# One of the last stores of a short-sequence attention kernel, sent out in three pieces of 49, 49 and 30 rows

## Chip, cores, metric

One core of one Trainium2 chip. The metric is device time in microseconds (us) of the whole program; each number is the median of several executions, or a single one where the text says so.

## The reference

```python
q, k, v: (32, 12, 128, 64) float32
scale = 1.0 / np.sqrt(q.shape[-1])
scores = scale * np.matmul(q, k.transpose(0, 1, 3, 2))
attn = np.exp(scores - scores_max)
attn = attn / (np.sum(attn, axis=-1, keepdims=True) + 1e-8)
return np.matmul(attn, v).astype(np.float32)
```

384 heads of 128 x 64. The kernel works in 24 chunks of 16 heads.

## The kernel before

A chunk's result is one tile in SBUF, the on-chip memory: 128 partitions (rows) with 4 KB each. Its store moves these 128 rows of 4 KB (512 KB) to HBM, the main memory. Stores are held back while loads run, and go out in groups of three at the end:

```python
def store(c, eng):
    o_sb, _ = osbs.pop(c)
    eng.dma_start(out=orr[:, c, :], in_=o_sb.rearrange("p t d -> p (t d)"))

e = NCH - 1                                   # 23
held = {c: [c - LAG] if c >= LAG else [] for c in range(e - 4)}
# ... (cut: held[e - 4] to held[e - 2])
held[e - 1] = [e - 5, e - 4, e - 3]           # stores 18, 19, 20
held[e] = [e - 2, e - 1, e]                   # stores 21, 22, 23
# ... (cut: the chunk loop)
    for s in held[c]:
        store(s, nc.scalar if s < e - 2 else nc.sync)
```

Stores up to 20 are issued from ScalarE, the last three from SyncE. Each store uses one of eight completion semaphores, in rotation, and waits until the store that had it before has landed. All loads but two at the start are issued from GpSimd and cast to bf16 on the way.

The softmax here doesn't subtract the row's maximum and nothing guards it: scores larger than these inputs give would overflow.

## Time and profile before

| | before |
|---|---|
| median | 130.61 us (130.34 to 130.7, 3 runs) |
| span of the profiled execution | 128.6 us |
| last exp on ScalarE | 114.95 to 116.84 us |
| stores 18, 19, 20 issued | 115.03, 115.47, 116.18 us |
| stores 21, 22, 23 issued | 114.62, 118.82, 121.92 us |
| last landing of store 23 | 127.35 us |

The prediction below shows the lines of this profile. The core has 16 DMA engines; a store of 128 rows gives 8 rows to each, and the store has landed when the slowest of the 16 is done. The engines reach SBUF through *ports*, each of which serves a group of partitions; the prediction names the page that tells of them.

Two things are read from the trace below the level of the page. *Landings* are the single semaphore increments, one for each DMA engine that a store used. *Row records* are the single 4 KB packets with start and duration; 159 ns is the usual one, and a *long record* here is one well above that. A new record of an engine starts 3 or 4 ns before its last one ends, so that records can be linked into one chain for each engine. That linking is a reconstruction: the ends of the chains are firm, while two chains may have been swapped further back. The tables of chains below therefore also ask that the rows between the increments of one queue fit the stores: 8 of a whole store, and 7, 7 and 2 of the three pieces.

### The profile page before, as it was taken

To read this page: it belongs to the slowest core of one execution; us is meant where nothing else is said; L and a number is where in the kernel's file an instruction comes from. 1 tells how busy PE (TensorE), PEld (TensorE's weight loads), DVE (VectorE), ACT (ScalarE), POOL (GpSimd) and SP (SyncE) were. 2 spreads that over 40 slices of the span, in tenths; PEclk is the share of its full clock that TensorE was granted. 3 is DMA by queue.
4 is the path that set the end of the run, shared out by engine and by line. 5 is a ranking of instruction groups with operands and counts; after the bars stand their busy time and mean duration, and the time that the engine had idled before them with its cause. 6 is when DMAs were issued, how large, how long until landed. Compare 5 with 4: busy or idle time off the path is not lost.

```text
span 128.6 us, 4637 instructions
## 1 busy us (share of the span) xinstructions
PE 69.7 (54%) x2080; PEld 42.7 (33%) x2080; DVE 85.7 (67%) x150; ACT 71.8 (56%) x74; POOL 79.5 (62%) x88
## 2 busy tenths in 40 slices
PE   0036966577546757775636296190976663684000
PEld 0025644444223433443314144050544331552000
DVE  0380398584879678979958669464799997777500
ACT  3216588669658737875774486371757775523000
POOL 6951314235699986998738487808999952355300
PEclk9999999999999977999999959968689998555555
DMA  3999999999999999999999999999999999999982
GB/s 118 312 194 186 210 204 204 209 213 202 216 202 209 207 215 206 207 212 209 283 290 269 221 284 207 286 287 209 287 210 285 287 285 325 389 418 414 419 364 83
DMA packets 16723, 32.27 MB, mean 251 GB/s; under 512 B 1344, under 2 KB 7488, under 8 KB 16704
## 3 DMA queue, kind: packets, MB, share of 16 engines
q0 software_dynamic: 12960, 18.35, 80.1%
q10 hardware_dynamic: 3168, 11.54, 23.0%
q1 hardware_dynamic: 576, 2.10, 4.2%
q8 instruction: 16, 0.26, 0.7%
q14 instruction: 3, 0.02, 0.0%
HBM read 37.75 MB, written 12.58 MB: 391 GB/s over the span
## 4 chain that ended last, share of the span: by engine, by line
DMA 58%; DVE 12%; POOL 11%; PE 6%; issue 4%; ACT 1%; POOLq 0%; DVEq 0%; ACTq 0%
DMA k_bf<-in_k_dram 33%; DMA q_bf<-in_q_dram 11%; DMA v_bf<-in_v_dram 11%; DVE o_sb L178 6%; POOL o_sb L183 4%; POOL v_bf L65 4%; PE s_ps L120 3%; DMA out_dram<-o_sb 3%; DVE kt L109 3%; DVE qt L107 2%; POOL q_bf L58 2%; PE o_ps L159 2%; ACT attn L124 1%; DVE o_sb L186 1%; PE v_ps L139 1%
## 5 line engine op out<-in xcount | busy, mean ns | idle before, releaser
L124 ACT ACTIVATE attn<-s_ps 128x2048 bf16<-128x2048 f32 x24 | 45.1, 1877 | 38.2 <-PE s_ps L120 33.2
L183 POOL TENSOR_TENSOR o_sb<-o_sb,recip 128x1024 f32<-128x1024 f32 x23 | 43.9, 1915 | 8.7 <-DVE o_sb L178 8.5
L178 DVE STREAM_TRANSPOSE o_sb<-o_ps 128x512 f32<-128x512 f32 x48 | 33.1, 711 | 14.3 <-PE o_ps L159 13.2
L139 PE MATMUL v_ps<-v_bf,perm 128*32 128x512 bf16 (+1 forms) x448 | 33.5, 405 | 3.4 <-DMA v_bf<-in_v_dram 3.4
L120 PE MATMUL s_ps<-qt,kt 32*128 32x128 bf16 x768 | 17.2, 232 | 33.1 <-DVE kt L109 33.1
L143 ACT CAST v<-v_ps 128x512 bf16<-128x512 f32 x48 | 26.4, 589 | 2.6 <-PE v_ps L139 2.4
L120 PEld LDWEIGHTS <-kt 32*128 32x128 bf16 x768 | 12.6, 100 | 43.1 <-DVE kt L109 42.5
L159 PE MATMUL o_ps<-attn,v 128*32 128x128 bf16 x768 | 22.4, 245 | 2.7 <-issue 2.7
L58 POOL DMA_DIRECT2D k_bf<-in_k_dram x23 | 12.3, 536 | 15.5 <-DMA v_bf<-in_v_dram 10.8
L171 DVE STREAM_TRANSPOSE dt<-d_ps 128x512 f32<-128x512 f32 x24 | 16.3, 678 | 6.4 <-PE d_ps L149 6.4
L109 DVE STREAM_TRANSPOSE kt<-k_bf 128x512 f32<-128x512 f32 x24 | 16.3, 680 | 5.5 <-DMA k_bf<-in_k_dram 5.4
L159 PEld LDWEIGHTS <-v 128*32 128x32 bf16 x768 | 15.7, 108 | 11.4 <-issue 6.5
L58 POOL DMA_DIRECT2D q_bf<-in_q_dram x23 | 13.5, 585 | 6.4 <-DMA v_bf<-in_v_dram 3.7
L107 DVE STREAM_TRANSPOSE qt<-q_bf 128x512 f32<-128x512 f32 x24 | 16.2, 673 | 1.6 <-DMA q_bf<-in_q_dram 1.5
L149 PE MATMUL d_ps<-attn,ones 128*32 128x512 bf16 x96 | 11.4, 453 | 9.5 <-ACT attn L124 9.5
L65 POOL DMA_DIRECT2D v_bf<-in_v_dram x12 | 9.1, 760 | 9.3 <-DMA k_bf<-in_k_dram 3.4
L139 PEld LDWEIGHTS <-perm 128*32 128x32 bf16 x448 | 12.1, 110 | 5.0 <-issue 2.6
L149 PEld LDWEIGHTS <-ones 128*32 128x32 bf16 x96 | 4.7, 104 | 15.8 <-issue 12.9
L173 DVE RECIPROCAL recip<-dt 128x16 f32<-128x16 f32 x24 | 6.1, 254 | 1.9
L83 DVE CAST q_bf<-raw 128x1024 bf16<-128x1024 f32 x1 | 0.8, 815 | 5.3 <-DMA raw<-in_q_dram 5.3
L83 ACT CAST k_bf<-raw 128x1024 bf16<-128x1024 f32 x1 | 1.0, 1046 | 3.0 <-DMA raw<-in_k_dram 3.0
L83 ACT ACT_TABLE_LOAD x1 | 1.3, 1283 | 1.2 <-PEq L244 1.2
(11 smaller groups left out, 3.8 us busy)
## 6 DMA issues: line engine op xcount, KB each, us to landing
out_dram<-o_sb ACTq DMA_DIRECT2D x21, 512.0 KB, 7.4
v_bf<-in_v_dram POOLq DMA_DIRECT2D x12, 512.0 KB, 13.8
q_bf<-in_q_dram POOLq DMA_DIRECT2D x23, 256.0 KB, 13.4
k_bf<-in_k_dram POOLq DMA_DIRECT2D x23, 256.0 KB, 13.2
out_dram<-o_sb SPq DMA_DIRECT2D x3, 512.0 KB, 6.4
raw<-in_k_dram ACTq DMA_DIRECT2D x1, 512.0 KB, 4.7
raw<-in_q_dram SPq DMA_DIRECT2D x1, 512.0 KB, 4.6
```

Of the source, the lines that this page charges most:

```text
L58: nc.gpsimd.dma_start(out=x, in_=src[:, c, :].rearrange("p (t d) -> p t d", t=TQ))
L107: nc.vector.transpose(xt.rearrange("p h (x g) -> p x h g", g=GQ), x)
L109: nc.vector.transpose(xt.rearrange("p h (x g) -> p x h g", g=GQ), x.rearrange("p (y t) e -> p t y e", y=2))
L120: nc.tensor.matmul(s_ps[:, b, h, :], lhsT=kt[pr, h, :, j], rhs=qt[pr, h, :, j], start=(j == 0), stop=(j == 1), tile_position=(b * 32, 0))
L124: nc.scalar.activation(out=attn, in_=s_ps, func=mybir.ActivationFunctionType.Exp, bias=0.0, scale=scale)
L139: nc.tensor.matmul(v_ps[u * 32:(u + 1) * 32, i], lhsT=perm[:, a + i, tl, :], rhs=v_bf[:, ns, 2 * u + tl, :], start=(tl == 0), stop=(tl == ...
L143: nc.scalar.copy(v2s[m][:, a:a + heads, ns], v_ps)
L149: nc.tensor.matmul(d_ps[b * 32:(b + 1) * 32], lhsT=ones, rhs=attns[c][:, b], start=True, stop=True, tile_position=(0, b * 32))
L159: nc.tensor.matmul(o_ps[b * 32:(b + 1) * 32, h], lhsT=v2s[c // 4][:, 4 * (b % 2) + h, 2 * (c % 4) + b // 2, j * 32:(j + 1) * 32], rhs=attn ...
L171: nc.vector.transpose(dt, turned(d_ps))
L178: nc.vector.transpose(o_sb[:, :, j * 32:(j + 1) * 32], turned(o_ps))
L183: nc.gpsimd.tensor_mul(o_sb, o_sb, recip.to_broadcast([128, TQ, D]))
```

## The change

The intent, as its sizes tell it: to take rows of one late store off the higher DMA engines and give them to the lower ones, so that all end together. It can be done only through the number of rows of a piece, because that number decides how many engines carry it.

```diff
+    UNEVEN = NCH - 4
@@
         def store(c, eng):
             o_sb, _ = osbs.pop(c)
-            eng.dma_start(out=orr[:, c, :], in_=o_sb.rearrange("p t d -> p (t d)"))
+            rows = (0, 49, 98, 128) if c == UNEVEN else (0, 128)
+            for lo, hi in zip(rows, rows[1:]):
+                eng.dma_start(out=orr[lo:hi, c, :],
+                              in_=o_sb[lo:hi].rearrange("p t d -> p (t d)"))
```

## The prediction

> **What bounds the kernel now.** I read the page's 40 slices first, then the engine busy times of the tail, then the waits of the SyncE queue, then the single landings of the last stores. In the slices the computing engines stop two to four slices before the end, while the DMA row stays full almost to the last slice (one slice is 128.6 / 40 = 3.2 us):
>
> ```profile
> DVE  0380398584879678979958669464799997777500
> ACT  3216588669658737875774486371757775523000
> POOL 6951314235699986998738487808999952355300
> PEclk9999999999999977999999959968689998555555
> DMA  3999999999999999999999999999999999999982
> ```
>
> The end is not compute: DVE and POOL end in slice 38 of 40. The tail cut into stretches (columns: stretch, its length, busy time of PE, PEld, DVE, ACT, POOL, granted clock, mean busy share of the 16 DMA engines, GB/s):
>
> ```profile
> 118.00:120.00 2.00, 0.35 (x15) 0.08 (x4) 1.86 (x5) 0.00 (x0) 1.47 (x2) 0.50 1.02 412
> 120.00:122.00 2.00, 0.00 (x0) 0.00 (x0) 0.92 (x1) 0.00 (x0) 0.37 (x1) 0.50 1.02 416
> 122.00:124.00 2.00, 0.00 (x0) 0.00 (x0) 0.00 (x0) 0.00 (x0) 0.00 (x0) 0.50 1.03 422
> 124.00:125.00 1.00, 0.00 (x0) 0.00 (x0) 0.00 (x0) 0.00 (x0) 0.00 (x0) 0.50 0.81 332
> 125.00:126.00 1.00, 0.00 (x0) 0.00 (x0) 0.00 (x0) 0.00 (x0) 0.00 (x0) 0.50 0.50 205
> 126.00:127.00 1.00, 0.00 (x0) 0.00 (x0) 0.00 (x0) 0.00 (x0) 0.00 (x0) 0.50 0.35 143
> 127.00:128.60 1.60, 0.00 (x0) 0.00 (x0) 0.00 (x0) 0.00 (x0) 0.00 (x0) 0.50 0.00 0
> ```
>
> No engine computes after 121 us; all 16 DMA engines are full until 124, then half of them (0.50), then a third, then none. So the last 3 us are an uneven finish, and the program ends only when the last store has landed:
>
> ```profile
> SPq L191 <- POOL o_sb L183: 17.4, 2, 13.6
> SPq L255 <- DMA out_dram<-o_sb: 4.9, 2, 4.0
> ```
>
> The second line is the closing wait of SyncE (a closing exchange of semaphores between the engines follows it, from the last landing at 127.35 to the end of the span at 128.6). The single semaphore increments of the last stores, one for each DMA engine, are in the trace; sorted, they fall into seven early, one in the middle and eight late (us from the span's start; stores numbered by chunk):
>
> | store | seven early | one | eight late |
> |---|---|---|---|
> | 19, ScalarE queue | 120.67 to 121.76 | 121.81 | 123.47 to 124.59 |
> | 20, ScalarE queue (the one changed) | 121.91 to 123.18 | 123.51 | 125.51 to 126.43 |
> | 23, SyncE queue (last) | 124.41 to 125.50 | 125.53 | 126.74 to 127.35 |
>
> The increments do not carry the engine's number. Seven early ones and a change that uses seven engines belong together: I take the early seven for engines 0 to 6. That is an inference, not a reading. A 4 KB row costs an engine 156 ns: increments of consecutive stores on one early engine lie 1,248 ns apart for 8 rows. The record of one row is 159 ns with sixteen engines running and the same 159 ns with eight, so the engines do not slow each other through a common limit.
>
> **What the Trainium skill says.**
> - "DMA: Bandwidth & Descriptors", section "Why a DMA increments its semaphore by 16 and not by 1": a store issued from ScalarE or SyncE uses the largest number up to 16 that divides its slowest dimension, on the lowest-numbered engines. So 49 rows go on engines 0 to 6 with 7 rows each, and 30 rows on 0 to 14 with 2 each. The trace agrees as far as it can: each 128-row store there shows 16 increments.
> - The same page, "Latency and other measured facts": engines 7 and 15 are usually the slower ones, by its best guess because of the descriptor rings of loads issued from GpSimd. The trace has the lag, but on eight engines, not two; it is there already when the last such loads land (104.7 to 109.3 us for one of them).
> - "SBUF — State Buffer", section "Door 1: The DMA port swizzle": rows 0 to 63 sit on eight ports and 64 to 127 on the other eight, a port gives about 27.2 GB/s, and it was measured that 64 partitions get hardly more than 32. One engine takes 4,096 / 156 ns = 26.3 GB/s here, so one engine nearly fills one port. The trace of before has no two engines on one port on purpose, so it can't show what sharing costs.
>
> **The change part by part.** It removes one 128-row store of 8 rows on each of 16 engines, and adds three.
> 1. *Rows by engine.* Engines 0 to 6: 7 + 7 + 2 = 16 rows, 8 more. Engines 7 to 14: 2 rows, 6 fewer. Engine 15: none, 8 fewer. Sum 7 x 16 + 8 x 2 = 128, as before.
> 2. *Ends.* Early engines: 8 x 0.156 = 1.25 us later, so 125.66 to 126.75. Late engines: 6 x 0.156 = 0.94 us earlier, 125.80 to 126.41 (engine 15 0.31 us more). The middle one, if it is engine 7, ends at 124.6. The last landing moves from 127.35 to 126.75: **0.60 us saved**. The rest of the closing, 1.25 us, stays.
> 3. *Two more issues.* One costs ScalarE's queue 0.34 us (median of its store issues). In the built kernel the first piece takes the semaphore of store 20, the second that of store 15, the third that of store 16, and each waits until that store has landed: at 117.32 and 118.74. ScalarE computes nothing after 116.84, so the issues cost no compute. The early engines still have stores 19 and the first piece to carry until after 121 us, so the pieces are in the ring some 2 us before they are due. **0 us.**
> 4. *The three last stores.* Their semaphores are the same ones in both builds; the last one waits for store 21 to land (121.85), which is ahead of store 20 on the late engines. **0 us.** On TensorE, VectorE and GpSimd the instructions are in the same order.
>
> Sum: 130.61 - 0.60 = 130.0 us if a row costs the same on any engine. I take a third of that off for shared ports (below): **130.2 us**.
>
> **Rivals.**
> - *Ports, not engines.* Rows 64 to 127 sit on the eight ports that the late engines read through. After the change an early engine reads up to 34 of those 64 rows from the second piece, and more from the third, at a time (121 to 124) when the late engines read there without a pause. If the port is the limit, the rows of each port are as many as before and the late half gains nothing; an early engine that shares takes up to twice 156 ns for some 5 to 7 rows, at most 1.1 us: end at 127.3 to 127.8, time 130.6 to 131.0. For it: the skill's measurement and 26.3 against 27.2 GB/s. Against it: nothing in this trace. I give it 35%.
> - *The early seven are not engines 0 to 6.* If late engines are among them, they get 8 rows more: 127.35 + 1.25 = 128.6, time 131.9. For it: no increment names its engine, and the grouping is one execution's. Against it: the sizes of the change fit the seven. 10%.
> - *A late issue.* The pieces wait for stores 15 and 16; were these some 3 us later, engines 0 to 6 would run dry. Then the change gives back part of its 0.6 us: 130.3. 5%.
> - The chunk pipeline before 116 us, where loads set the pace, is not touched; a gain of more than 1.3 us could only come from there.
>
> **Range and chances.** The engine sum gives 130.0 (about half), the port rival 130.6 to 131.0, the wrong seven 131.9. The runs of before differ by 0.36 us. So 129.6 to 131.1 holds about 8 in 10. Two per cent is 2.6 us, twice the largest effect counted on either side: faster 0.02, same 0.95, slower 0.03.
>
> **What would show it.** Right: the DMA share of 124 to 126 rises from 0.5 to 0.8 or more, and falls to nothing by 126.8 instead of 127; the last store's landings close up, engine 7 apart, to a spread of about 1.1 us from 2.9; rows still take 159 ns. Ports: row records of 200 to 320 ns between 121 and 126, and the last landing at 127.3 or later. Wrong seven: a longer tail at a share of 0.5 or less. Late issue: a gap on seven engines, with full share lost before 124. The prediction fails if the load phase shifts between builds, so that stores begin their tail at another time than 116 us.

## The result and the profile after

| | before | after |
|---|---|---|
| median | 130.64 us (130.34 to 130.7, 4 runs) | 131.62 us (131.42 to 131.94, 4 runs) |
| ratio | 1 | 1.0082 (95%: 1.0055 to 1.0108) |
| last landing of store 23 | 127.35 us | 128.43 us |
| store 23 issued | 121.92 us | 121.90 us |
| row time beyond 159 ns a row, all engines, from 117 us | 0.6 us | 8.1 us |

A ratio is the mean time of one kernel's fast runs over that of the other's of the same rounds, so not quite the ratio of the medians. The kernel became about 0.8% slower, where 0.3% faster was forecast; 131.62 us is above the range of 129.6 to 131.1 us.

The tail of the changed kernel in the same stretches (stretch, length, busy time of PE, PEld, DVE, ACT, POOL, granted clock, mean busy share of the DMA engines, GB/s):

```profile
118.00:120.00 2.00, 1.16 (x36) 0.82 (x28) 1.54 (x4) 0.00 (x0) 1.60 (x1) 0.50 1.03 410
120.00:122.00 2.00, 0.00 (x0) 0.00 (x0) 1.69 (x2) 0.00 (x0) 1.04 (x1) 0.50 0.99 381
122.00:124.00 2.00, 0.00 (x0) 0.00 (x0) 0.00 (x0) 0.00 (x0) 0.00 (x0) 0.50 0.99 354
124.00:125.00 1.00, 0.00 (x0) 0.00 (x0) 0.00 (x0) 0.00 (x0) 0.00 (x0) 0.50 1.05 389
125.00:126.00 1.00, 0.00 (x0) 0.00 (x0) 0.00 (x0) 0.00 (x0) 0.00 (x0) 0.50 0.77 315
126.00:127.00 1.00, 0.00 (x0) 0.00 (x0) 0.00 (x0) 0.00 (x0) 0.00 (x0) 0.50 0.26 107
127.00:128.00 1.00, 0.00 (x0) 0.00 (x0) 0.00 (x0) 0.00 (x0) 0.00 (x0) 0.50 0.16 66
128.00:129.70 1.70, 0.00 (x0) 0.00 (x0) 0.00 (x0) 0.00 (x0) 0.00 (x0) 0.50 0.00 0
```

Part of the forecast is there: the share in 125 to 126 us rose from 0.50 to 0.77, and in 126 to 127 it fell from 0.35 to 0.26. Two things were not foreseen. From 127 to 128 us a share of 0.16 stays, two to three engines of sixteen. And between 120 and 124 us the engines are as busy as before (0.99) but move 381 and 354 GB/s, where before moved 416 and 422: busy time that moves less, which is what long row records look like in this view. The closing wait of SyncE for the last stores (us in total, times, longest) grew with it, from 4.9 us:

```profile
SPq L194 <- POOL o_sb L184: 17.7, 2, 14.0
SPq L259 <- DMA out_dram<-o_sb: 6.0, 2, 3.1
```

So two suspects stood at the start: **some of engines 0 to 6 are late ones** (called "wrong seven" in the expectations), and **shared SBUF ports**, which make rows long. Two more were kept as rivals: the two added issues with their semaphores, and the HBM side (an engine writes other output rows than before). The load phase did move a little between the two profiles: the last exp started at 115.76 us, 0.8 us later than before. The halves below show what that is worth: their last exp started at 115.74 us, and they end as before.

### The profile page after: what moved, and what is told of

The parts are those of the page before. It is cut to its first block, busy times and chain, and to the rows that moved or that the text cites. A ratio compares the mean times of both kernels' runs of the same rounds, so it can differ in the third digit from the quotient of the medians.

```text
span 129.7 us, 4639 instructions
## 1 busy us (share of the span) xinstructions
PE 70.6 (54%) x2080; PEld 42.9 (33%) x2080; DVE 85.3 (66%) x150; ACT 71.7 (55%) x74; POOL 79.6 (61%) x88
## 4 chain that ended last, share of the span: by engine, by line
DMA 58%; DVE 12%; POOL 11%; PE 7%; issue 3%; ACT 1%; ACTq 0%; POOLq 0%; DVEq 0%
DMA k_bf<-in_k_dram 34%; DMA q_bf<-in_q_dram 11%; DMA v_bf<-in_v_dram 11%; DVE o_sb L179 6%; POOL o_sb L184 4%; POOL v_bf L66 4%; PE s_ps L121 4%; DVE kt L110 3%; DMA out_dram<-o_sb 3%; DVE qt L108 2%; POOL q_bf L59 2%; PE o_ps L160 2%; ACT attn L125 1%; DVE o_sb L187 1%; PE v_ps L140 1%
## 5 line engine op out<-in xcount | busy, mean ns | idle before, releaser
L121 PE MATMUL s_ps<-qt,kt 32*128 32x128 bf16 x768 | 17.7, 237 | 33.0 <-DVE kt L110 33.0
L144 ACT CAST v<-v_ps 128x512 bf16<-128x512 f32 x48 | 26.3, 590 | 2.9 <-PE v_ps L140 2.9
L66 POOL DMA_DIRECT2D v_bf<-in_v_dram x12 | 9.3, 775 | 10.6 <-DMA k_bf<-in_k_dram 4.6
```

Source lines behind the costliest of these rows:

```text
L121: nc.tensor.matmul(s_ps[:, b, h, :], lhsT=kt[pr, h, :, j], rhs=qt[pr, h, :, j], start=(j == 0), stop=(j == 1), tile_position=(b * 32, 0))
L144: nc.scalar.copy(v2s[m][:, a:a + heads, ns], v_ps)
```

## The experiments

All kernels but one (nine more stores at the end) differ from the changed kernel, or from the one before, only in how store 20 (in one group stores 18 to 20) is cut, and three of them in the partitions that it reads. Those with a wrong result are named.

### Which part of the loss is issue, which is ports

**Columns.** Three pieces again, but each with all 128 rows, so that engines and ports are as before:

```diff
-            rows = (0, 49, 98, 128) if c == UNEVEN else (0, 128)
+            cols = (0, 6, 12, 16) if c == UNEVEN else (0, 16)
+            # out=orr[:, c, lo * D:hi * D], in_=o_sb[:, lo:hi]
```

> Store 20 in three pieces by columns (6, 6 and 4 of the 16 groups of 64): all 128 rows in each piece, so each engine keeps its own port and its own share, and only the number of issues and semaphores is that of the change. Shared ports, HBM side or counts as the cause: 130.5 to 130.9 us. Issue and semaphores: 131.4 to 131.9 us.

Measured: 130.76 us, 1.000 (0.9978 to 1.0022). Two more issues and their semaphores cost nothing that can be measured. That rival is out.

**Halves.** Every engine has its 8 rows, but two engines read through one port:

```diff
-            rows = (0, 49, 98, 128) if c == UNEVEN else (0, 128)
+            rows = (0, 64, 128) if c == UNEVEN else (0, 128)
```

> Store 20 as rows 0 to 63 and 64 to 127: each half over all 16 engines with 4 rows each, so every engine has 8 rows as before, but two engines read through one port. Shared ports: records of about 300 ns in both halves, time 130.9 to 131.8 us. Counts of rows by engine as the cause: 130.6 us, records of 159 ns. Issue and semaphores as the cause: about half the loss, 131.1 us, without long records.

Measured: 130.74 us, 1.0011 (0.998 to 1.0042). Long records are there (4.9 us beyond 159 ns in all, up to 639 ns), but the last landing is 127.46 us, as before. Its tail ends before 127.0 us, as before:

```profile
125.00:126.00 1.00, 0.00 (x0) 0.00 (x0) 0.00 (x0) 0.00 (x0) 0.00 (x0) 0.50 0.64 258
126.00:127.00 1.00, 0.00 (x0) 0.00 (x0) 0.00 (x0) 0.00 (x0) 0.00 (x0) 0.50 0.39 160
127.00:128.60 1.60, 0.00 (x0) 0.00 (x0) 0.00 (x0) 0.00 (x0) 0.00 (x0) 0.50 0.00 0
```

Shared ports alone, with equal rows, did not move the end. The expectation from ports missed.

**Even and odd ports.** The three pieces of the change, to the same output rows, but all read from partition 0 on, or all from partition 64 on (wrong results):

```diff
             for lo, hi in zip(rows, rows[1:]):
+                f = 0 if c == UNEVEN else lo        # second kernel: f = 64
                 eng.dma_start(out=orr[lo:hi, c, :],
-                              in_=o_sb[lo:hi].rearrange("p t d -> p (t d)"))
+                              in_=o_sb[f:f + hi - lo].rearrange("p t d -> p (t d)"))
```

> The same three pieces of store 20 on the same engines and to the same rows of the output, but each piece is read from the lowest SBUF partitions (0 to 48, 0 to 48, 0 to 29), so nothing of it is read from partitions 64 to 127. The result is wrong on purpose. If shared SBUF ports are the cause: the long row records (300 to 700 ns) mostly go, the late eight engines end some 0.9 us earlier than in before, and the time is 130.0 to 130.8 us, at or below before. If the cause is on the HBM side (which output rows an engine writes), or the counts of rows by engine, or the later issue of the pieces: as the change, 131.4 to 131.9 us.

> The same, but each piece is read from partition 64 on (64 to 112, 64 to 112, 64 to 93), so all 128 rows come through the eight ports that the late engines use. Wrong on purpose. Shared ports: those ports carry 8 rows more on average, the fullest 12 more, so the end is 1.2 to 1.9 us or more later than before, 132 to 133 us, with many records above 300 ns. HBM side, counts or issue: as the change, 131.4 to 131.9 us.

Measured: 131.70 us, 1.0096 (1.0035 to 1.0156) with partition 0 on; 133.06 us, 1.0175 (1.0147 to 1.0202) with partition 64 on. The first one was to bring the gain if the upper eight ports were the cause. It did not: its tail keeps the share of 0.16 to the same end:

```profile
125.00:126.00 1.00, 0.00 (x0) 0.00 (x0) 0.00 (x0) 0.00 (x0) 0.00 (x0) 0.50 0.84 332
126.00:127.00 1.00, 0.00 (x0) 0.00 (x0) 0.00 (x0) 0.00 (x0) 0.00 (x0) 0.50 0.33 123
127.00:128.00 1.00, 0.00 (x0) 0.00 (x0) 0.00 (x0) 0.00 (x0) 0.00 (x0) 0.50 0.16 66
```

The two kernels write the same output rows from the same engines and differ by 1.4 us, so that difference is on the SBUF side, and it is a matter of ports: 20.2 us of row time beyond 159 ns against 4.5 us. The kernel that reads from partition 64 on, in its tail:

```profile
122.00:124.00 2.00, 0.00 (x0) 0.00 (x0) 0.39 (x1) 0.00 (x0) 0.00 (x0) 0.50 0.98 326
124.00:126.00 2.00, 0.00 (x0) 0.00 (x0) 0.00 (x0) 0.00 (x0) 0.00 (x0) 0.50 0.98 297
126.00:128.00 2.00, 0.00 (x0) 0.00 (x0) 0.00 (x0) 0.00 (x0) 0.00 (x0) 0.50 0.46 164
128.00:130.00 2.00, 0.00 (x0) 0.00 (x0) 0.00 (x0) 0.00 (x0) 0.00 (x0) 0.50 0.13 53
```

I read the full share (0.98) at 297 GB/s as the sign of shared ports. They can cost time, then, when they are loaded enough; but the end of the change itself does not come from the upper ports.

### A shared port by itself

Nine more stores of chunk 22's rows after the last one, each waiting for the one before it (cut: a change to `store` that keeps the tile):

```diff
+        o_sb, _ = osbs[e - 1]
+        for lo, hi in ((0, 128), (64, 128), (0, 128), (0, 64), (0, 49),
+                       (0, 128), (49, 98), (0, 128), (98, 128)):
+            nc.sync.dma_start(out=orr[lo:hi, e - 1, :],
+                              in_=o_sb[lo:hi].rearrange("p t d -> p (t d)"))
```

> After the last store nine more stores of chunk 22's rows (the same data to the same place), one after the other: rows 0 to 127, 64 to 127, 0 to 127, 0 to 63, 0 to 48, 0 to 127, 49 to 97, 0 to 127, 98 to 127. It measures a shared port by itself. If two engines on one port share its rate, the records of 64 to 127 and 0 to 63 are near 300 ns, against 159 ns in 0 to 127, and half of the rows take as long as all. If engines are the limit, they stay at 159 ns. Time some 25 us longer.

Measured (153.11 us as a whole; the time isn't of interest):

| rows | engines | first record's start to last one's end | median row record |
|---|---|---|---|
| 0 to 127 | 16 | 1.44 us | 161 or 162 ns |
| 64 to 127 | 16 | 1.40 us | 319 ns |
| 0 to 63 | 16 | 1.41 us | 319 ns |
| 0 to 48 | 7 | 1.78 us | 159 ns, up to 452 |
| 49 to 97 | 7 | 1.54 us | 159 ns, up to 312 |
| 98 to 127 | 15 | 0.73 us | 250 ns |

Rows 64 to 127 (the first line), rows 0 to 127 and rows 0 to 63, in the stretches:

```profile
129.90:131.30 1.40, 0.00 (x0) 0.00 (x0) 0.00 (x0) 0.00 (x0) 0.00 (x0) 0.50 0.88 187
132.55:134.00 1.45, 0.00 (x0) 0.00 (x0) 0.00 (x0) 0.00 (x0) 0.00 (x0) 0.50 0.89 359
135.50:136.90 1.40, 0.00 (x0) 0.00 (x0) 0.00 (x0) 0.00 (x0) 0.00 (x0) 0.50 0.81 173
```

Half of the rows, from half of the ports, take as long as all of them, at half the rate, with all engines busy. So two engines on one port share its rate. The two pieces of 49 rows take 1.78 and 1.54 us where 7 rows of 156 ns would be 1.09. So the long records of the changed kernel have an explanation; what remained was whether they set the end.

### Which engines are late

A piece of k rows goes to the k lowest engines, one row each, so its landings are theirs alone. Three kernels cut stores 18, 19 and 20 into k, 16 - k and 112 rows, and two more cut store 20 alone:

```diff
+            first = {18: 1, 19: 3, 20: 7}.get(c)    # and {18: 2, 19: 4, 20: 8}, {18: 5, 19: 6, 20: 7},
+                                                    # {20: 7}, {20: 5}
+            rows = (0, 128) if first is None else (0, first, 16, 128)
```

> Which engines are the early and the late ones. Stores 18, 19 and 20 go out as a first small piece, the rest of 16 rows, and 112 rows: 1 + 15 + 112, 3 + 13 + 112 and 7 + 9 + 112. A piece of k rows gives one row to each of the k lowest engines, so its landings are theirs alone. If the early seven are engines 0 to 6, the pieces of 1, 3 and 7 rows land only at early times (some 2 us before the late group of the same store). If some of engines 0 to 6 are late, the piece of 7 shows as many late landings, three by my reading of the changed kernel's first piece. Time within 130.4 to 131.2 us.

> The same with 2 + 14 + 112, 4 + 12 + 112 and 8 + 8 + 112. Early seven = engines 0 to 6: no late landing in the pieces of 2 and 4, at most one in that of 8. Otherwise the counts, with those of the other two kernels, tell which engines are late.

> The same with 5 + 11 + 112, 6 + 10 + 112 and 7 + 9 + 112. Early seven = engines 0 to 6: no late landing in the pieces of 5, 6 and 7. Otherwise counts as above.

> Store 20 as 7 + 9 + 112 rows, the other stores whole: the 7 landings of the first piece are those of engines 0 to 6, right behind store 19. Early seven = engines 0 to 6: all within 1.5 us of the early landings of store 19. Wrong seven: two to four of them after the first late landing of store 19. Time 130.4 to 130.9 us.

> The same as 5 + 11 + 112. Wrong seven, with engines 0 to 3 early: four early landings in the piece of 5, and one in the middle or late; four late ones in the piece of 11. Time 130.4 to 130.9 us.

Measured: 132.25, 130.53, 131.98, 130.38 and 130.84 us (one run each). The times of the first and third miss what was expected (the fourth by 0.02 us): with nine pieces on eight semaphores the last pieces were issued only at 124 to 126 us, so several of the small pieces tell nothing. Pieces of 1, 2, 3, 6 and 10 rows, left out of the table, are in line with it. Those that landed in time and tell most:

| piece | landings early or middle | landings late | compared with |
|---|---|---|---|
| 4 rows | 120.50 to 120.62 (4) | none | store 18's rest: late from 121.71 |
| 5 rows | 121.78, 121.95, 122.01, 122.08; middle 122.61 | none | store 19: early to 121.66, middle 122.42, late from 123.44 |
| 7 rows | 121.15, 121.39, 121.74, 121.97; middle 122.27 | 123.41, 123.45 | store 19: early to 121.64, middle 122.08, late from 123.21 |
| 9 rows | 7 landings to 122.46 | 123.72, 123.73 | the same store 19 |
| 11 rows | 7 landings to 122.80 | 4 landings from 123.75 | the store 19 of the piece of 5 |
| 12, 13, 14, 15 rows | 7 each | 5, 6, 7, 8 | store 18 or 19 of the same kernel |

Read from row to row, each step adds one engine. **Engines 0 to 3 are early, 4 is the middle one, 5 and 6 are late, 7 and 8 early, 9 to 14 late**, and what is left for engine 15 is the seventh early place. There are seven early engines, as the prediction said, but they are not the lowest seven. (No trace names an engine; that a piece of k rows goes to the k lowest-numbered ones is taken over from the prediction.) These traces come from two chips; the first pieces of the changed kernel, in three traces on further occasions, have again four landings at early times, one in between (in one trace just behind the early ones) and two later.

### Rows on the four early engines

Row counts alone would make this better: 17 rows on engines 0 to 3, 4 rows on engines 0 to 14, so no late engine gets more than before. The second kernel reads from partition 0 on (wrong):

```diff
-            rows = (0, 49, 98, 128) if c == UNEVEN else (0, 128)
+            rows = (0, 68, 128) if c == UNEVEN else (0, 128)
```

> Store 20 as rows 0 to 67 (17 each on engines 0 to 3) and 68 to 127 (4 each on engines 0 to 14). By the landings of the three probes engines 0 to 3 are early, and the late ones are among 4 to 14. Wrong seven as the cause: every late engine has 4 rows fewer (0.62 us), engines 0 to 3 have 13 more (2.03 us, to 126.4 to 127.5), so the end is 126.7 to 127.5 and the time 130.0 to 130.7 us, faster than the change by about 1 us. Shared ports as the cause: the eight upper ports still carry all their 64 rows, and two pieces share ports as in the change: 131 us or more.

> The same with both pieces read from partition 0 on, so at most 4 rows come through the upper eight ports. Wrong on purpose. Wrong seven alone: the same time as with all ports, 130.0 to 130.7 us. If the upper ports hold the late engines back in the kernel above, this one is faster than it by up to 0.5 us.

Measured: 132.64 us for the first: its profiled execution took 130.48 us, the other five 132.34 to 133.93 us (four of these count as slow, because they are over 1.5% above the fastest; three of them show a TensorE clock of 0.81, but so does an execution of the kernel before that took 130.62 us). 132.42 us (131.79 to 133.42), 1.0132 (1.0097 to 1.0168), for the second. Both miss the 130.0 to 130.7 us of row counts alone. I saw two explanations left: other engines are late from one execution to the next, or shared ports. Three more traces of the first kernel, and one of the changed kernel:

> The kernel of e_low4 again, unchanged, for a second trace. If the late engines are other ones from execution to execution: a slow execution (132.3 us or more) has one or more of the four landings of its piece of 68 rows on an engine whose store 19 landed late, and that engine ends last without long row records. If slow executions come from shared ports: engines 0 to 3 are early again and the engine that ends last has several microseconds of row time beyond 159 ns a row.

> The same as the one before, a third trace of the same kernel. Either theory expects of it what is told there.

> The same again, a fourth trace of the same kernel. Either theory expects of it what is told for the second trace.

> The changed kernel again, unchanged, for a second trace. Wrong seven: 131.4 to 131.9 us, two to four engines end last, some 1.2 us after the other late ones, with little or no row time beyond 159 ns a row; their number may differ from three. Shared ports: the engines that end last are those with the most long records.

Measured: 132.89, 133.51 and 133.09 us, and 133.61 us for the changed kernel, above what row counts alone had been expected to give. In all three of the slow traces two or three of the four landings of the piece of 68 rows come at 124.41 to 125.64 us, which only an early engine can reach: a late one, done with store 19 at 123.3 us or later, needs 17 x 0.156 = 2.65 us more. The row time beyond 159 ns is 7.4 to 10.6 us in the slow traces and 2.5 us in the fast one. The fast execution first:

```profile
120.00:122.00 2.00, 0.00 (x0) 0.00 (x0) 0.38 (x1) 0.00 (x0) 0.00 (x0) 0.50 1.02 418
122.00:124.00 2.00, 0.00 (x0) 0.00 (x0) 0.00 (x0) 0.00 (x0) 0.00 (x0) 0.50 0.97 385
124.00:126.00 2.00, 0.00 (x0) 0.00 (x0) 0.00 (x0) 0.00 (x0) 0.00 (x0) 0.50 0.83 326
126.00:128.00 2.00, 0.00 (x0) 0.00 (x0) 0.00 (x0) 0.00 (x0) 0.00 (x0) 0.50 0.15 59
```

and a slow one of the same kernel:

```profile
120.00:122.00 2.00, 0.00 (x0) 0.00 (x0) 1.97 (x3) 0.00 (x0) 1.15 (x2) 0.50 0.98 369
122.00:124.00 2.00, 0.00 (x0) 0.00 (x0) 0.24 (x1) 0.00 (x0) 0.00 (x0) 0.50 0.96 336
124.00:126.00 2.00, 0.00 (x0) 0.00 (x0) 0.00 (x0) 0.00 (x0) 0.00 (x0) 0.50 0.98 365
126.00:128.00 2.00, 0.00 (x0) 0.00 (x0) 0.00 (x0) 0.00 (x0) 0.00 (x0) 0.50 0.28 113
128.00:130.00 2.00, 0.00 (x0) 0.00 (x0) 0.00 (x0) 0.00 (x0) 0.00 (x0) 0.50 0.08 33
```

The slow one is as busy between 120 and 124 us and moves 369 and 336 GB/s instead of 418 and 385. So I read the slow executions as shared ports, with most of the four engines in their usual early places; that the fourth one was early too isn't shown. Nor is it shown that the engines that end last are those with several microseconds of long records, as had been expected of shared ports: under the conditions named above their chains can't be followed back. What puts an execution in one or the other group stays open: in the fast one the last exp started at 114.42 us, in the slow traces at 116.03 to 116.27, so the pieces met the other stores at other moments, but one fast trace is no proof. In none of its executions did this kernel clearly beat the one before.

### Half the dose

> About half the change: rows 0 to 48, 49 to 112 and 113 to 127 of store 20, so engines 0 to 6 get 7 + 4 + 1 = 12 rows (4 more than before), engines 7 to 14 get 5 and engine 15 gets 4. Late engines among the seven as the cause: they end up to 4 x 0.156 = 0.62 us later than in before, so 130.9 to 131.4 us, and 1.003 to 1.005 of before, half of the full change run beside it. If the loss is a fixed cost of uneven pieces, it is that of the full change. If half the shift suits the early engines, it is below before.

> The changed kernel again, timed on the same chip as the half change. 131.4 to 131.9 us if it repeats its first result, about 1.2 to 1.3 us after before at most from the count of rows alone. Its fourth earlier run beside e_low4 took 133.61 us, so a spread upward, to 133.6 us, would show that shared ports add to it in some executions or on some chips.

```diff
-            rows = (0, 49, 98, 128) if c == UNEVEN else (0, 128)
+            rows = (0, 49, 113, 128) if c == UNEVEN else (0, 128)
```

Measured on one chip: 131.11 us (130.77 to 132.38), 1.0055 (1.0024 to 1.0085), with 4 rows more on engines 0 to 6; 132.14 us (131.41 to 133.55, the last one not counted as fast), 1.0096 (1.0072 to 1.0120), with 8 more. About half the dose gives about half the loss, within wide intervals. The changed kernel's spread is larger than in its first four runs.

The tail of the half dose, for comparison with the 0.26 and 0.16 of the full change in its first trace:

```profile
126.00:127.00 1.00, 0.00 (x0) 0.00 (x0) 0.00 (x0) 0.00 (x0) 0.00 (x0) 0.50 0.38 156
127.00:128.00 1.00, 0.00 (x0) 0.00 (x0) 0.00 (x0) 0.00 (x0) 0.00 (x0) 0.50 0.01 4
```

Which engines end last, and with how much row time beyond 159 ns since 119.5 us, from records linked under the conditions named above. A dash marks a chain that can't be followed back under them:

| execution | last chains: end (us), time in long records (us) |
|---|---|
| before | eight, 126.39 to 127.01; 0.00 each |
| changed kernel, first trace | 127.82, 0.00; 127.88, 0.00; 128.02, - |
| changed kernel, timed last | 127.65, 0.00; 127.93, 0.00 |
| changed kernel, 133.61 us | 128.19, -; 129.06, 0.44; 130.07, - |
| pieces read from partition 0 on | 127.83, -; 127.83, 0.00; 128.09, 0.00 |
| half the dose | 127.16, 0.00; 127.30, 0.00 |

Row counts say for a late engine with 8 rows more: 126.39 to 127.01 plus 1.25, so 127.64 to 128.26; with 4 more, 127.01 to 127.63. Two engines end there in both of the faster traces of the change, in the kernel that reads from partition 0 on, and with half the dose, and none of them has a long record. The chains say who they are, too: they hold 7, 7 and 2 rows of store 20 (7, 4 and 1 with half the dose), as only engines 0 to 6 do, and their increment of store 19 comes between 122.6 and 123.4 us, with the late ones. By the probes that is engines 5 and 6. Rows of 159 ns on these engines also leave no room for the HBM side at this end. In the first trace a third engine ends with them; its first piece landed at 124.45 us, between the early and the late ones, which fits engine 4, but why it ended so late is not settled. In the 133.61 us execution the one of the last three that can be followed has long records as well.

## Why the prediction was wrong

- *The bound, right.* The end of the span is the last landing of store 23 plus 1.25 us before and 1.27 us after.
- *Rows by engine, right.* The first piece shows one early increment for the engines it does not use, and then seven landings. The relief worked, too: in the first trace of the change the late engines that were not among the seven have their last landings among those at 126.23 to 126.42 us, where the prediction had 125.80 to 126.41.
- *Ends, wrong, and this is the step that failed:* "I take the early seven for engines 0 to 6." The early ones are 0 to 3, 7, 8 and 15. Engines 5 and 6 are late, and 8 more rows put the ends of their records at 127.65 to 127.93 us; the last landing came at 128.43 us (128.28 in the trace timed last) in place of the 126.75 us predicted. The inference was circular: the sizes of the change were taken as evidence of the thing that the change needs to be true. The seven was the right count in the trace, by chance, and it made the guess look firmer. The prediction listed this as its second rival with 10% and 131.9 us; the measured 131.62 us and the tail at a share of 0.16 are that rival's course.
- *Two more issues at no cost, right:* 130.76 us with three pieces of columns.
- *The last three stores not touched, right:* store 23 was issued at 121.90 us against 121.92 (store 22 0.8 us later than before, with the load phase).
- *The port rival, partly right.* Sharing is real (1.40 us for half the rows, against 1.44 us for all), and long records reach 720 ns in the first trace of the change and 1,015 ns in the slowest, well above the "up to twice 156 ns" of the prediction. Its premise that the late engines are those of rows 64 to 127 rests on the same wrong grouping. But with the upper ports out of use the loss stayed (131.70 us), and the two late engines end last without long records. It is not the cause of the first 1 us. That it is what adds to it in some executions, up to 133.61 us, is likely but not shown by a run of its own.
- *"A late issue" did not happen:* the pieces were issued at 116.99, 118.40 and 119.54 us, ahead of their turn.

## What to carry to other kernels

A grouping of landings in a trace says how many engines are late, not which; before rows are shifted between DMA engines, send a few pieces of k rows and count. Cutting a 128-row store so that engines read each other's partitions makes rows long even when row counts are balanced (4.9 us in all in the halves, though there the end did not move). A late engine need not be a slow one: when nothing else runs, the 16 landings of a whole store come within 0.18 us (128.54 to 128.72 us, the first of the nine more stores), and in the kernel before the lag is about as large at store 12 (110.67 to 111.38 us against 112.30 to 113.58) as at store 23. The late engines come out of the load phase behind and then keep pace. A change that needs a hidden fact to hold is no evidence for that fact.

## What the Trainium skill lacked or had wrong

- "DMA: Bandwidth & Descriptors", section "Latency and other measured facts", has engines 7 and 15 as the usually slower ones. Here engine 7 was among the early and, by what the counts leave, engine 15 too; 5, 6 and 9 to 14 were late, by 2 to 3 us (store 19 landed at 120.67 to 121.76 us on the early seven, at 123.47 to 124.59 us on the late eight). I found no page with such a pattern, and no run here shows its cause.
- The same page, section "Why a DMA increments its semaphore by 16 and not by 1", is borne out: pieces of 4, 5, 7, 9 and 11 rows gave as many landings, and the counts fit nested sets of engines. What it lacks is a way to use that: landings of such pieces as a probe of single engines.
- "SBUF — State Buffer", section "Door 1: The DMA port swizzle", is borne out for stores: 64 rows took 1.40 us and 128 rows 1.44. It lacks what that means for odd splits: 49 rows over seven engines took 1.78 and 1.54 us, where seven rows of 156 ns would be 1.09; and that single row records reach 319 ns (two engines on a port, alone) and 1,071 ns (with other stores under way, all read from partition 64 on).
- "DMA: Bandwidth & Descriptors", section "Specifications", gives about 27 GiB/s for one engine, which is 29.0 GB/s; a 4 KB row took an engine 156 ns here, 26.3 GB/s.
